# Two chunks of a small projection placed between the chunks of the first input block

## The chip, the cores and the metric

The kernel runs on one core of a Trainium2 chip. The metric is the device time in microseconds of one execution, the median of several runs. The engines are TensorE (PE, with its weight loads listed apart as PEld), VectorE (DVE), ScalarE (ACT), GpSimd (POOL) and SyncE (SP), which here only starts transfers (DMAs).

## The reference

One decoder layer on 256 tokens of width 2048, all in float32:

```
h = rms_norm(x);  proj = h @ w_in            # 2048 x 10536, split into mLSTM, RWKV-7 and gate columns
x = x + rms_norm(merge(mlstm(...), rwkv7(...), gates) @ w_out)
x = x + rms_norm(cross_attention(rms_norm(x), rms_norm(mem)))
x = x + rms_norm((gelu(conv(h @ w_up)[gate]) * conv(h @ w_up)[up]) @ w_down)     # 2048 -> 2 x 8192 -> 2048
```

Of the columns of `w_in`, 296 are a small projection: the low-rank inputs of RWKV's decay, rate and gate (64, 64 and 160 columns) and the 8 gate columns of the mLSTM heads. The rest is a matter of large matrix products.

## The kernel before

**Blocks and chunks.** All large products are cut into blocks, listed in `blocks` in the order in which they run, and each block into chunks along the contraction. In an "fm" block (512 output columns) the weights are the stationary operand and the activations (256 tokens) the moving one; a chunk is two slices of 128 rows, 1024 values on each of the 128 partitions (512 KB). In a "tm" block the activations are stationary. The float32 product is made of three passes with two-part operands: activations high and low (`hh`, `hl`), weights high and low (`wh`, `wl`), as high x high, low x high and high x low. So an fm chunk is 2 x 4 x 3 = 24 matmuls of 256 columns; a chunk of the small projection (block 1, "tm", 296 columns, 8 chunks, 296 KB each) is 12 matmuls of 296 columns.

**Order and indices.** `visits()` lists which chunks of which block run when; the running number of a chunk in that list, `i`, is its index. Before: 0 to 7 the first input block (`w_in` 0), 8 to 15 the small projection, 16 to 71 seven more fm input blocks, 72 to 103 four tm blocks, 104 to 199 gates and branches, 200 to 231 the mixer's output, 232 to 239 the key block of cross-attention, 240 and 241 the first two chunks of its value block, 242 to 249 its query block, 250 to 255 the rest of the value block, 256 to 263 its output block, 264 to 519 the up projection (32 blocks), 520 to 647 the down projection.

**Feed.** `Feed` loads and stages the chunks by index. `dma` starts the load on SP; `hi` casts the chunk to the high part on ACT (L401); `lo` subtracts on DVE (L441). Each index is staged a few indices ahead of its matmuls (`feed.lo(i + 3)`, loads up to `i + 6`). The first eight indices land in a space of their own (`sm`), the others in a ring of four. `begin`, `first` and `second` do the same by hand for the first two chunks, in halves. For the first block the activations themselves are loaded in pieces of two slices (`x_load`, 256 KB each) and split into `hh` and `hl` by `x_piece` (ACT and DVE, L66), called from `pre_r0`. Loads are queued on SP in program order. Each engine works through its instructions in program order too.

**Line place and kicks.** `staged` chooses where in its buffer the staged weights of a chunk start: 16 elements in for fm blocks and for blocks narrower than 512 columns, 0 for wider tm blocks, the two slices `e` elements apart. The table `KICK` displaces single indices by 8 elements: kind 0 the first slice, kind 1 the second, kind 2 both. It costs no instruction.

**Side work.** What is not a chunk (evacuations of finished blocks, statistics, attention, the RWKV recurrence) is written as generators which `Spread` serves in small pieces. Its step, `half()`, is called twice in each chunk; it takes at most one piece of the first-come queue, as a budget for ACT and DVE allows, and the pieces of the "chains", which come each `chain` steps, the first after `phase` steps. Pieces that have matmuls or transposes put them into PE's stream between two half chunks; such an insertion is called a visit here. The first block's evacuation contains the statistic of the first norm; the small block's evacuation ends with six transposes and starts the gates and the low-rank work. `x_tokens` (L1939 to L1948) is a chain that transposes the residual for the final output: 32 transposes of 128 x 128, four to each of eight visits, with one copy by ACT behind each visit, 8 steps (four chunks) apart.

Of the kernel before, what the change touches and what calls it, by code (L numbers as in the profile page):

```python
# [15 lines left out]
P = 128  # L16
# [129 lines left out]
def _layer(ctx, tc, nc, d, dbg):  # L146
    act, dve = Meter(nc.scalar, 200.0, 0.83), Meter(nc.vector, 70.0, 1.04)
    pool, pe, sp = nc.gpsimd, nc.tensor, nc.sync
    side = Spread(act, dve)
# [27 lines left out]
    def aux(name, shape=None):  # L177
        return pp.tile(shape or [P, 512], F32, tag="aux", bufs=4, name=name)
# [157 lines left out]
    blocks = []  # L336

    def block(kind, srcs, xs, evac, before=None, cols=512, pool_=None, pre=None, bankwise=False, tail=0):
# [2 lines left out]
                           pool=pool_ or acc, pre=pre, task=None, bankwise=bankwise, tail=tail))  # L341
        return blocks[-1]

    KICK = {16: 0, 18: 2, 36: 2, 52: 1, 60: 2, 104: 0, 108: 0, 111: 0, 116: 0, 117: 1, 120: 1, 134: 0, 138: 2, 140: 0, 159: 1,
            168: 0, 216: 2, 219: 2, 236: 2, 243: 2, 257: 2, 266: 2}

    HB = [slice(0, 256), slice(256, 512)]

    class Feed:
# [7 lines left out]
        def begin(self):  # L357

            r = self.raw[0] = self.sm[0][:, 0]
            m = KD + S  # L360
            sp.dma_start(xf[:, 0:m], d["xf"][:, 0:m])
            act.dma_start(r[:, 0, HB[0]], self.src[0][:, 0, HB[0]])
            sp.dma_start(r[:, 0, HB[1]], self.src[0][:, 0, HB[1]])
            act.dma_start(r[:, 1], self.src[0][:, 1])
            sp.dma_start(xf[:, m:], d["xf"][:, m:])
            r = self.raw[1] = self.sm[0][:, 1]
            for j in range(2):
                sp.dma_start(xq[1][:, j], d["x"][:, 2 + j])
                sp.dma_start(r[:, j], self.src[1][:, j])
            act.activation(mhalf[:, 0:1], mhalf[:, 0:1], AF.Copy)  # L370
            self.nd = 2

        def dma(self, upto):
            while self.nd <= min(upto, len(self.src) - 1):
                s = self.src[self.nd]
                if self.nd < 8:
                    r = self.sm[self.nd // 4][:, self.nd % 4]
                else:
                    r = wp.tile(list(s.shape), F32, tag="raw", bufs=4, name="raw")
                sp.dma_start(r, s)  # L380
                self.raw[self.nd] = r
                self.nd += 1

        def staged(self, name, r, i):


            k, c = r.shape[1:]
            kick = KICK.get(i)
            e = -(-c // 64) * 64
            o = 0 if c >= 512 and self.kind[i] == "tm" else 16  # L390
            if kick is not None:
                o, e = ((24, e + 24), (o, e + 8), (24, e))[kick]
            w = wp.tile([P, 1024 + 128], F32R, tag=name, bufs=4, name=name)
            return w[:, o:o + k * e].rearrange("p (k c) -> p k c", k=k)[:, :, 0:c]
# [10 lines left out]
        def first(self):  # L405

            r, wh, wl = self.raw.pop(0), self.staged("wh", self.src[0], 0), self.staged("wl", self.src[0], 0)
            for h in HB:
                nc.vector.tensor_copy(wh[:, 0, h], r[:, 0, h])
            for kj in range(2):  # L410
                x_split(0, kj)
                if kj:
                    nc.scalar.copy(wh[:, 1], r[:, 1])
                nc.vector.tensor_sub(wl[:, kj], r[:, kj], wh[:, kj])
            self.st[0] = [wh, wl]

        def second(self):

            r, wh, wl = self.raw.pop(1), self.staged("wh", self.src[1], 1), self.staged("wl", self.src[1], 1)
            for kj in range(2):  # L420
                x_split(1, kj)
                nc.scalar.copy(wh[:, kj], r[:, kj])
                nc.vector.tensor_sub(wl[:, kj], r[:, kj], wh[:, kj])
            self.st[1] = [wh, wl]
            self.ns = self.nl = 2

        def early(self, i):

# [33 lines left out]
    def visits():  # L462

        out = []
        for b in blocks:
            n = len(b["srcs"])
            if b is xv:
                out.append((b, 0, 2))
            elif b is xq_:
                out += [(b, 0, n), (xv, 2, len(xv["srcs"]))]  # L470
            elif b is entry[0]:
                out += [(v, c, c + 1) for c in range(n) for v in entry]
            elif b is not entry[1]:
                out.append((b, 0, n))
        return out

    def run():
        order = visits()
        feed = Feed([("xv" if b is xv else b["kind"], s) for b, c0, c1 in order for s in b["srcs"][c0:c1]])
        feed.begin()  # L480
        for c in range(2, 8):
            x_load(c)
            feed.dma(c)
            if c == 4:
                sp.dma_start(par, d["par"])
        i = 0
        pend, ring = [], []
        for b, c0, c1 in order:
            if c0 == 0:
# [4 lines left out]
                n = (b["cols"] // P + 1) // 2 if b["kind"] == "fm" else 2 * max(1, b["cols"] // 512)  # L494
                b["banks"], b["k"] = [], 0
                for _ in range(n):
# [4 lines left out]
                    o = b["pool"](b["kind"], [P, 2, S] if b["kind"] == "fm" or b is xv else None)  # L501
# [3 lines left out]
            banks, nm, k = b["banks"], b["cols"] // P, b["k"]  # L505
# [5 lines left out]
                srcs, tail = srcs[:-nt], srcs[-nt:]  # L511
            for ci, s in enumerate(srcs):
                if b["pre"]:
                    b["pre"](ci, feed)
                feed.lo(i + 1)
                twin = bool(entry) and ci == 0 and c0 == 0 and b in entry
                if twin and b is entry[0]:
# [7 lines left out]
                wh, wl = feed.st.pop(i)  # L525
                for kj in range(s.shape[1]):
                    xh, xl = b["xs"](k) if kj else ahead
                    first, last = k == 0, k == nk - 1
                    if b["kind"] == "fm":
                        steps = []  # L530
                        for m in range(nm):
                            o = banks[m // 2][:, m % 2]
                            a, c = wh[:, kj, m * P:(m + 1) * P], wl[:, kj, m * P:(m + 1) * P]
# [19 lines left out]
                    else:  # L553
                        for g, o in enumerate(banks):
                            n = o.shape[1]
# [9 lines left out]
            if nt:  # L565
# [10 lines left out]
                n = len(steps)  # L576
# [49 lines left out]
    def x_piece(c):  # L626
        for j in range(2):
            x_split(c, j)
# [4 lines left out]
    def pre_r0(ci, feed):  # L633
        if ci == 0:
            keep_warm(7)
            feed.first()
            feed.second()
            x_piece(2)
            feed.lo(2)
        if ci + 3 < 8:  # L640
            x_piece(ci + 3)
        else:

            for c in range((ci - 5) * 2, (ci - 5) * 2 + 2):
                st0.add(xq[c])
        if ci == 4:
            sp.dma_start(con, d["con"])

    def pre_sm(ci, feed):
        if ci == 0:  # L650
            sp.dma_start(up[0:64], d["w_up"])
        if ci == 1:
            sp.dma_start(up[64:128], d["a_up"])

    M, tasks = {}, {}
# [1192 lines left out]
    def fu_evac(b):  # L1848
        def gen(ps):
# [17 lines left out]

            if b == 0:
                yield from M["res"].wait(30)
                side.add(x_tokens(), chain=8)  # L1870
            dve.tensor_mul(us[0], ps[0], bc(stf.rb, 2))
            yield
            base(0)
# [62 lines left out]
    def x_tokens():  # L1936

        M["xt"] = []
        for f in range(4):  # L1939
            if f % 2 == 0:  # L1940
                M["xt"].append(U("xt", [P, 2, 1024]))
            for t in range(2):
                q = aux("xt", [P, 4, P])
                for j in range(4):
                    k = f * 4 + j
                    pe.transpose(q[:, j], M["xr"][k // 8][:, k % 8, t * P:(t + 1) * P], ident)  # L1946
                act.copy(M["xt"][f // 2][:, t, f % 2 * 512:f % 2 * 512 + 512], q.rearrange("p a b -> p (a b)"))
                yield  # L1948

    def load_gain():  # L1950
        M["gain"] = mp.tile([P, D], F32, tag="hT", bufs=2, name="gain")
# [175 lines left out]
```

## Time and profile before

| | |
|---|---|
| median of 3 runs | 1863.75 us (1863.1 to 1864.75) |
| the profiled execution | 1862.86 us, span 1861.0 us |
| PE / PEld busy | 1851.9 / 1767.3 us |
| DVE / ACT / POOL busy | 1296.2 / 1015.3 / 34.8 us |
| granted TensorE clock | 0.999 |
| read from HBM | 347.01 MB, 188 GB/s over the span |

A row of the timeline is: start in us from the span's start, duration in us, engine, line of the kernel, operation, output tile <- input tiles, shapes, and the number of merged instructions; in brackets idle time of the engine before it and who ended it. `fm` and `tm` are the PSUM tiles of blocks of these kinds. Matmuls are pipelined: the distance from start to start counts, not the duration. Staged weights and the activations have the names `wh`, `wl`, `hh`, `hl` (in later blocks `mh`, `qh`, `fh` and so on). The DMA view lists transfers by line with their size and the median time from issue to landing.

### The profile page before, as it was taken

What the parts mean: (1) busy time and instruction counts of PE and PEld (TensorE: products, weight loads), DVE (VectorE), ACT (ScalarE), POOL (GpSimd) and SP (SyncE); (2) the same over time, 40 slices, a digit from 0 to 9 for tenths busy, and PEclk for the clock granted to TensorE, in tenths of its full rate; (3) what the DMA queues carried; (4) which work ended last, traced back from release to release, by engine and by line L of the source; (5) the groups of instructions that cost most, each with busy time, mean ns of one, the idle gap of its engine ahead of it and who ended that gap; (6) DMA issues with size and microseconds to landing.
All of it is one profiled execution on the core that took longest, in us unless ns stands there. A gap on an engine that the chain in (4) does not pass through costs nothing.

```text
span 1861.0 us, 36212 instructions
## 1 busy us (share of the span) xinstructions
PE 1851.9 (100%) x14930; PEld 1767.3 (95%) x14930; DVE 1296.2 (70%) x1834; ACT 1015.3 (55%) x1493; POOL 34.8 (2%) x64
## 2 busy tenths in 40 slices
PE   9999999999999999999999999999999999999998
PEld 9999888999999999999999999999999988888887
DVE  7889787566676858787766667766666775556555
ACT  6776445555454746666554455444445554545544
POOL 0100020000000000000000000000000000000000
PEclk9999999999999999999999999999999999999999
DMA  7556545455556765555666666666666666666664
GB/s 263 192 174 192 181 153 163 133 164 156 177 190 195 273 203 182 161 183 172 197 196 195 196 193 193 192 193 195 195 196 194 195 193 215 192 193 192 194 192 145
DMA packets 98486, 351.47 MB, mean 189 GB/s; under 512 B 10960, under 2 KB 11984, under 8 KB 97936
## 3 DMA queue, kind: packets, MB, share of 16 engines
q1 hardware_dynamic: 97744, 348.23, 59.8%
q8 instruction: 117, 1.92, 0.4%
q10 hardware_dynamic: 576, 0.92, 0.1%
q14 instruction: 49, 0.40, 0.1%
HBM read 347.01 MB, written 2.10 MB: 188 GB/s over the span
## 4 chain that ended last, share of the span: by engine, by line
PE 99%; DMA 0%; DVE 0%; ACT 0%; issue 0%; DVEq 0%; ACTq 0%
PE fm L181 69%; PE tm L181 25%; DMA w<-in_w_in_dram 0%; PE gram L181 0%; PE Y L181 0%; PE num L181 0%; PE lv L181 0%; PE X L181 0%; PE U L181 0%; PE zg L181 0%; PE zwa L181 0%; PE xsc L181 0%; PE xt L1946 0%; PE stb L181 0%; PE Tn L181 0%; PE xo L181 0%
## 5 line engine op out<-in xcount | busy, mean ns | idle before, releaser
L441 DVE TENSOR_TENSOR wl<-raw,wh 128x1024 fp32r<-128x1024 f32 (+1 forms) x639 | 774.9, 1218 | 415.3 <-ACT wh L401 407.6
L401 ACT CAST wh<-raw 128x1024 fp32r<-128x1024 f32 (+1 forms) x639 | 663.9, 1044 | 472.7 <-PE fm L181 358.7
L181 PE MATMUL fm<-fh,wh 128*128 128x256 f32 x2048 | 565.4, 277 | 0.6 <-DVE fh L66 0.6
L181 PE MATMUL fm<-fl,wh 128*128 128x256 f32 x2048 | 564.4, 277 | 0.0
L181 PE MATMUL fm<-fh,wl 128*128 128x256 f32 x2048 | 564.4, 277 | 0.0
L181 PEld LDWEIGHTS fm<-fh,wh 128*128 128x128 f32 x2048 | 383.9, 188 | 0.8 <-DVE fh L66 0.8
L181 PEld LDWEIGHTS fm<-fl,wh 128*128 128x128 f32 x2048 | 383.8, 188 | 0.0
L181 PEld LDWEIGHTS fm<-fh,wl 128*128 128x128 f32 x2048 | 383.7, 188 | 0.0
L181 PE MATMUL tm<-wh,as 128*128 128x512 f32 x1024 | 315.6, 390 | 0.0
L181 PE MATMUL fm<-hh,wh 128*128 128x256 f32 x1024 | 284.5, 280 | 0.7 <-ACT wh L401 0.6
L181 PE MATMUL fm<-hh,wl 128*128 128x256 f32 x1024 | 282.1, 277 | 0.8 <-DVE wl L441 0.8
L181 PE MATMUL fm<-hl,wh 128*128 128x256 f32 x1024 | 282.0, 277 | 0.0
L181 PEld LDWEIGHTS tm<-wh,as 128*128 128x128 f32 x1024 | 192.2, 188 | 39.9
L181 PE MATMUL tm<-wl,as 128*128 128x512 f32 x512 | 199.5, 390 | 0.0
L181 PEld LDWEIGHTS fm<-hh,wh 128*128 128x128 f32 x1024 | 192.2, 189 | 1.7 <-ACT wh L401 0.8
L181 PEld LDWEIGHTS fm<-hh,wl 128*128 128x128 f32 x1024 | 191.5, 188 | 1.0 <-DVE wl L441 1.0
L181 PEld LDWEIGHTS fm<-hl,wh 128*128 128x128 f32 x1024 | 191.7, 188 | 0.1
L181 PEld LDWEIGHTS tm<-wl,as 128*128 128x128 f32 x512 | 96.1, 188 | 19.9
L66 ACT CAST as<-ac 128x256 fp32r<-128x256 f32 x128 | 45.6, 404 | 110.8 <-PE tm L181 110.8
L66 DVE TENSOR_TENSOR as<-ac,as 128x256 fp32r<-128x256 f32 x128 | 48.6, 421 | 61.7 <-ACT as L66 61.7
L181 PE MATMUL fm<-mgh,wh 128*128 128x256 f32 x256 | 71.1, 278 | 0.0
L181 PE MATMUL fm<-mgl,wh 128*128 128x256 f32 x256 | 70.9, 277 | 0.0
(411 smaller groups left out, 2224.5 us busy)
## 6 DMA issues: line engine op xcount, KB each, us to landing
raw<-in_w_fu_dram SPq DMA_DIRECT2D x256, 512.0 KB, 4.3
raw<-in_w_in_dram SPq DMA_DIRECT2D x152, 512.0 KB, 3.5
raw<-in_w_fd_dram SPq DMA_DIRECT2D x128, 512.0 KB, 4.0
raw<-in_w_br_dram SPq DMA_DIRECT2D x32, 512.0 KB, 4.2
raw<-in_w_mo_dram SPq DMA_DIRECT2D x32, 512.0 KB, 3.8
raw<-in_w_xk_dram SPq DMA_DIRECT2D x8, 512.0 KB, 3.6
raw<-in_w_xv_dram SPq DMA_DIRECT2D x8, 512.0 KB, 3.6
raw<-in_w_xq_dram SPq DMA_DIRECT2D x8, 512.0 KB, 4.0
```

The source lines that it names most:

```text
L66: return f(out, *a, **k)
L181: pe.matmul(out, lhsT, rhs, start=start, stop=stop, skip_group_check=True)
L401: nc.scalar.copy(wh, r)
L441: nc.vector.tensor_sub(wl, r, self.st[self.nl][0])
```

## The change

The first two chunks of the small projection move from indices 8 and 9 to 1 and 3: the order is now first block's chunk 0, small 0, chunk 1, small 1, chunks 2 to 7, small 2 to 7. From index 16 on all is as before. The loads, the casts and the splitting of x are reordered to match; the loads now run up to index 9 in `run` (the first eight indices' space holds the smaller chunks too). The small chunks' staged weights start at 0 instead of 16 elements. `con` and `up` are loaded at the same chunks of their blocks.

In `KICK` four entries go to the index ahead (138 to 137, 216 to 215, 236 to 235, 243 to 242; all of kind 2) and one is new (282).

`x_tokens` makes eight transposes and two copies in each of four visits, 16 steps apart, the first 24 steps after the point where it was before.

```diff
-    KICK = {..., 134: 0, 138: 2, 140: 0, 159: 1,
-            168: 0, 216: 2, 219: 2, 236: 2, 243: 2, 257: 2, 266: 2}
+    KICK = {..., 134: 0, 137: 2, 140: 0, 159: 1,
+            168: 0, 215: 2, 219: 2, 235: 2, 242: 2, 257: 2, 266: 2, 282: 2}
...
-            r = self.raw[1] = self.sm[0][:, 1]
+            self.nd = 1
+            self.dma(1)
+            r = self.raw[2] = self.sm[0][:, 2]
             for j in range(2):
                 sp.dma_start(xq[1][:, j], d["x"][:, 2 + j])
-                sp.dma_start(r[:, j], self.src[1][:, j])
+                sp.dma_start(r[:, j], self.src[2][:, j])
...
-            self.nd = 2
+            self.nd = 3
...
-            o = 0 if c >= 512 and self.kind[i] == "tm" else 16
+            o = 0 if self.kind[i] == "tm" else 16
...
-            if b is xv:
+            if b is blocks[0]:
+                out += [(b, 0, 1), (blocks[1], 0, 1), (b, 1, 2), (blocks[1], 1, 2), (b, 2, n)]
+            elif b is blocks[1]:
+                out.append((b, 2, n))
+            elif b is xv:
...
+        feed.dma(3)
         for c in range(2, 8):
             x_load(c)
-            feed.dma(c)
+            feed.dma(c + 2)
...
-            feed.second()
-            x_piece(2)
-            feed.lo(2)
-        if ci + 3 < 8:
-            x_piece(ci + 3)
+            feed.lo(1)
+            feed.second()
+            feed.lo(3)
+        elif ci < 5:
+            x_piece((0, 3, 5, 6, 7)[ci])
...
     def pre_sm(ci, feed):
-        if ci == 0:
+        if ci < 2:
+            x_piece(2 + 2 * ci)
+        if ci == 2:
             sp.dma_start(up[0:64], d["w_up"])
-        if ci == 1:
+        if ci == 3:
...
-                side.add(x_tokens(), chain=8)
+                side.add(x_tokens(), chain=16, phase=24)
...
-            for t in range(2):
-                q = aux("xt", [P, 4, P])
+            qs = [aux("xt", [P, 4, P]) for _ in range(2)]
+            for t, q in enumerate(qs):
                 for j in range(4):
                     k = f * 4 + j
                     pe.transpose(q[:, j], M["xr"][k // 8][:, k % 8, t * P:(t + 1) * P], ident)
+            for t, q in enumerate(qs):
                 act.copy(M["xt"][f // 2][:, t, f % 2 * 512:f % 2 * 512 + 512], q.rearrange("p a b -> p (a b)"))
-                yield
+            yield
```

More of the change, by code (lines that the diff above doesn't have):

```diff
@@ L342, in block @@
         return blocks[-1]
-    KICK = {16: 0, 18: 2, 36: 2, 52: 1, 60: 2, 104: 0, 108: 0, 111: 0, 116: 0, 117: 1, 120: 1, 134: 0, 138: 2, 140: 0, 159: 1,
-            168: 0, 216: 2, 219: 2, 236: 2, 243: 2, 257: 2, 266: 2}
+    KICK = {16: 0, 18: 2, 36: 2, 52: 1, 60: 2, 104: 0, 108: 0, 111: 0, 116: 0, 117: 1, 120: 1, 134: 0, 137: 2, 140: 0, 159: 1,
+            168: 0, 215: 2, 219: 2, 235: 2, 242: 2, 257: 2, 266: 2, 282: 2}
     HB = [slice(0, 256), slice(256, 512)]
@@ L376, in dma @@
                 if self.nd < 8:
-                    r = self.sm[self.nd // 4][:, self.nd % 4]
+                    r = self.sm[self.nd // 4][:, self.nd % 4].rearrange("p k c -> p (k c)")
+                    r = r[:, 0:2 * s.shape[2]].rearrange("p (k c) -> p k c", k=2)
                 else:
@@ L415, in first @@
             self.st[0] = [wh, wl]
+            self.ns = self.nl = 1
         def second(self):
-            r, wh, wl = self.raw.pop(1), self.staged("wh", self.src[1], 1), self.staged("wl", self.src[1], 1)
+            r, wh, wl = self.raw.pop(2), self.staged("wh", self.src[2], 2), self.staged("wl", self.src[2], 2)
             for kj in range(2):
@@ L423, in second @@
                 nc.vector.tensor_sub(wl[:, kj], r[:, kj], wh[:, kj])
-            self.st[1] = [wh, wl]
-            self.ns = self.nl = 2
+            self.st[2] = [wh, wl]
+            self.ns = self.nl = 3
         def early(self, i):
@@ L513, in run @@
                 if b["pre"]:
-                    b["pre"](ci, feed)
+                    b["pre"](c0 + ci, feed)
                 feed.lo(i + 1)
```

## The prediction

> **What bounds the kernel now.** I read the page first, for the engine that sets the span.
>
> ```profile
> span 1861.0 us, 36212 instructions
> PE 1851.9 (100%) x14930; PEld 1767.3 (95%) x14930; DVE 1296.2 (70%) x1834; ACT 1015.3 (55%) x1493; POOL 34.8 (2%) x64
> ```
>
> TensorE (PE) is busy for all but 9.1 us of 1861.0. Neither the matmuls nor their sizes are changed, so the change can only win or lose in PE's idle time and in the distance from one matmul's start to the next. The profiled execution took 1862.86 us, 1.86 us around its span, and the median of the runs shown is 1863.75, 0.89 us above it; the sum is made at 1862.86, and 0.89 us are added at the end.
>
> Next I read the timeline of the first 17 us, PE, ScalarE (ACT) and VectorE (DVE) apart, to find the idle time that the reordering can reach.
>
> ```profile
> 7.89 0.28 PE L181 MATMUL fm<-hh,wh 128*128 128x256 f32 x1
> ...
> 10.15 0.62 PE L181 MATMUL fm<-hh,wl 128*128 128x256 f32 x4
> 11.35 0.38 PE L181 MATMUL fm<-hh,wh 128*128 128x256 f32 x1 [0.58 <-ACT wh L401]
> 11.57 0.28 PE L181 MATMUL fm<-hl,wh 128*128 128x256 f32 x1
> 12.61 0.38 PE L181 MATMUL fm<-hh,wl 128*128 128x256 f32 x1 [0.76 <-DVE wl L441]
> ...
> 15.23 0.28 PE L181 MATMUL fm<-hh,wh 128*128 128x256 f32 x1
> ```
> ```profile
> 7.96 0.62 ACT L422 CAST wh<-w 128x512 fp32r<-128x512 f32 x1 [0.28 <-DMA w<-in_w_in_dram]
> ...
> 10.25 1.05 ACT L401 CAST wh<-w 128x1024 fp32r<-128x1024 f32 x1 [0.35 <-DMA w<-in_w_in_dram]
> ...
> 14.68 1.05 ACT L401 CAST wh<-w 128x1024 fp32r<-128x1024 f32 x1 [0.25 <-DMA w<-in_w_in_dram]
> ```
> ```profile
> 11.33 1.23 DVE L441 TENSOR_TENSOR wl<-w,wh 128x1024 fp32r<-128x1024 f32 x1 [0.92 <-ACT wh L401]
> ```
>
> The row at 7.89 is the first matmul of chunk 1 of the first input block, 11.35 that of chunk 2, 15.23 that of chunk 3. Chunk 2 waits twice: for its weights' cast, and at its third matmul for the subtraction. The cast at 10.25 itself waited for the transfer. From 10.25 a fixed chain runs to the third matmul at 12.61 (1.05 us cast, 1.23 us subtraction, some 0.08 between), 2.36 us. So **DMA sets the time up to 12.61**; after that PE runs without a stop while the casts still follow the transfers. The windows say the same (stretch, length, busy time of PE, PEld, DVE, ACT and POOL with counts, granted clock, DMA share, GB/s):
>
> ```profile
> 5.00:10.00 5.00, 4.91 (x41) 4.70 (x41) 4.25 (x9) 3.88 (x8) 0.00 (x0) 1.00 0.97 315
> 10.00:15.00 5.00, 3.66 (x30) 3.26 (x29) 3.78 (x7) 4.05 (x7) 0.00 (x0) 1.00 1.02 393
> ```
>
> DMA is full (0.97, 1.02), PE is not (3.66 of 5 us), and the granted clock is 1.00.
>
> **Part one, the small chunks moved forward.** Everything stands against the price of one small chunk, and of its casting:
>
> ```profile
> 28.83 0.30 PE L181 MATMUL tm<-wh,hh 128*128 128x296 f32 x1
> ...
> 30.43 0.29 PE L181 MATMUL tm<-wh,hh 128*128 128x296 f32 x1
> ```
> ```profile
> L441 DVE TENSOR_TENSOR wl<-raw,wh 128x592 fp32r<-128x592 f32 x4 | 3.1, 769 | 0.0
> ...
> L401 ACT CAST wh<-raw 128x592 fp32r<-128x592 f32 x4 | 2.7, 675 | 0.4 <-PE fm L181 0.4
> ```
>
> Twelve matmuls in 1.60 us, fed by 296 KB; a chunk of the input block takes 24 matmuls and needs 768 KB (512 of weights, 256 of x). Two small chunks bring PE 3.20 us of work that x chunk 0 and 1 already allow, and 592 KB that are queued on SP ahead of chunk 2. Two chunks' worth, 1536 KB, came between the casts at 10.25 and 14.68 (4.43 us, 347 KB/us), one chunk's 768 KB between 7.96 and 10.25 (335 KB/us). At 341 KB/us the 592 KB cost 1.73 us: the cast of chunk 2 moves from 10.25 to 11.98, and its third matmul to 11.98 + 2.36 = 14.34. Is PE there by then? From 7.89: small chunk 1.60, chunk 1 2.72 (the later spacing of 24 matmuls, priced below), small chunk 1.60 gives 13.81, two matmuls later 14.04. It still waits 0.3 us, once. From the third matmul to chunk 3 the trace has 15.23 - 12.61 = 2.62 us, so chunk 3 starts at 16.96, with 3.20 us of the later work done: as if at 13.76 instead of 15.23. **Gain 1.47 us.** Without the remaining wait it would be 1.77, and with the 0.1 us of restart (0.38 us for the matmul at 12.61 against 0.28) some 1.9. If the extra bytes come at the 315 GB/s of the window, 606 thousand bytes take 1.92 us and the gain is 1.28; if the small pieces land half a microsecond later still, some 0.8. I take 1.47.
>
> What else this step issues: the cast and subtraction of the first small chunk (0.68 and 0.77 us) come ahead of chunk 1's x and weights on ACT and DVE. Chunk 1's last weights, cast at 7.96 now, land 296/341 = 0.87 us later, at 8.83; cast 0.62 us and subtraction of like size end near 10.1, and PE needs that half at 7.89 + 1.60 + 1.36 = 10.85: covered. The chunks 3 and 4 of the block are cast one visit later in program order, but their transfers still lead PE: the cast of chunk 4, at 14.68 now, goes to 16.4 and its subtraction ends near 18.7, before 16.96 + 2.72 = 19.68. The loads of con, up and the other small chunks are queued later on SP, behind the block's own weights, for uses after 19 us. No wait is added beyond the one at 14.34.
>
> The Trainium skill, SBUF — State Buffer, section "The DMA setup-cost knee", gives 436 GB/s as the asymptote of large transfers; by it the 606 thousand bytes cost an estimated 1.39 us, no wait but a few hundredths is left, and the part would give 1.8 us.
>
> **Part two, the line place of the small chunks.** Their staged weights start at offset 0 instead of 16 elements, for all eight. No row has that form. Bounds: at the pace of the input blocks (2.72 us for 24 x 256 columns) 296 columns take 0.131 us against 1.60/12 = 0.133, a gain of 0.2 us over 96 matmuls; at the slow spacing described next, 4% dearer, a loss of 0.5. I take 0, nearest to a row that has the same shape.
>
> **Part three, the kick table.** An entry displaces one chunk's staged weights by 8 elements. What it acts on is seen by the first matmuls of successive chunks: rows of the cross-attention query block (indices 242 to 244 and the one behind), of the mixer's gates (137, 138, 139), of the key block (235, 236, 237), and chunk 18 with 19:
>
> ```profile
> 730.52 0.28 PE L181 MATMUL fm<-qh,wh 128*128 128x256 f32 x1
> ...
> 733.35 0.28 PE L181 MATMUL fm<-qh,wh 128*128 128x256 f32 x1
> ...
> 736.17 0.28 PE L181 MATMUL fm<-qh,wh 128*128 128x256 f32 x1
> ...
> 738.88 0.28 PE L181 MATMUL fm<-qh,wh 128*128 128x256 f32 x1
> ```
> ```profile
> 428.22 0.39 PE L181 MATMUL fm<-hh,wh 128*128 128x256 f32 x1
> ...
> 431.17 0.28 PE L181 MATMUL fm<-hh,wh 128*128 128x256 f32 x1
> ...
> 433.98 0.28 PE L181 MATMUL fm<-hh,wh 128*128 128x256 f32 x1
> ```
> ```profile
> 710.90 0.28 PE L181 MATMUL fm<-mh,wh 128*128 128x256 f32 x1
> ...
> 714.11 0.28 PE L181 MATMUL fm<-mh,wh 128*128 128x256 f32 x1
> ...
> 716.92 0.28 PE L181 MATMUL fm<-mh,wh 128*128 128x256 f32 x1
> ```
> ```profile
> 48.78 0.28 PE L181 MATMUL fm<-hh,wh 128*128 128x256 f32 x1
> ...
> 51.67 0.28 PE L181 MATMUL fm<-hh,wh 128*128 128x256 f32 x1
> ```
>
> Nothing waits in these stretches, yet 24 matmuls take 2.83, then 2.82 (the chunk with the kick), then 2.71. **There are two spacings**, 0.113 and 0.118 us; a visit of other matmuls or a change of block can leave PE in the slow one, 0.11 us a chunk, and a kicked chunk ends it. At 242 the kick now sits on the first slow chunk instead of the second: 2.83 + 2.82 becomes 2.82 + 2.71, gain 0.12. At 137 the slow chunk has a visit in front (2.95); a kicked chunk behind a visit takes 2.94 (172.18 to 175.12, quoted below), so 137 stays and 138 goes from 2.81 to 2.72: 0.09. I give 215 the same 0.09 as an estimate, being built like 137. At 235 the visit falls in the middle: 3.21 us, with a fast first half. A kick in fast spacing is dear (chunk 18: 51.67 - 48.78 = 2.89, 0.17 over 2.72), half of it 0.085, so 235 loses what 236 (2.81) wins: 0. The new one at 282 replaces the visit that ended the slow spacing there: 0. Sum 0.30; bounds 0 (the early kick doesn't hold and the slow spacing goes on, then more is lost, see the rivals) and 0.4.
>
> **Part four, the transposes.** Eight visits of four become four visits of eight, from chunk 295 instead of 283 on.
>
> ```profile
> 868.16 0.60 PE L1946 MATMUL xt<-con,xr 128*128 128x128 f32 x4
> 868.52 0.37 PE L181 MATMUL fm<-fh,wh 128*128 128x256 f32 x1
> 868.73 0.28 PE L181 MATMUL fm<-fl,wh 128*128 128x256 f32 x1
> 868.85 0.28 PE L181 MATMUL fm<-fh,wl 128*128 128x256 f32 x1
> 868.96 0.28 PE L181 MATMUL fm<-fh,wh 128*128 128x256 f32 x1
> ```
> ```profile
> 171.39 1.03 PE L1057 MATMUL vt<-con,vT 128*128 128x128 f32 x8
> 172.18 0.36 PE L181 MATMUL fm<-hh,wh 128*128 128x256 f32 x1
> ...
> 175.12 0.29 PE L181 MATMUL fm<-hh,wh 128*128 128x256 f32 x1
> ```
>
> The return to the stream costs 0.21 instead of 0.113 us, 0.10 a visit, the same behind four transposes as behind eight (172.18 against 868.52). Four visits less: **0.39 us**. ACT copies 2 x 0.59 us at once, with the whole up projection as cover, and the results are wanted only at the very end. The two PSUM banks of a visit are free, because the third block, which holds two of that pool, is evacuated before chunk 295.
>
> **Sum.** 1.47 + 0 + 0.30 + 0.39 = 2.16 us: 1862.86 - 2.16 = 1860.70, and with 0.89 a median of **1861.6**. That is 0.12% faster; a measurement of this kernel can tell about 0.2% (3.7 us) from no change.
>
> **Rivals.**
>
> *Eight transposes leave PE slow for good* (slower). The place is chunk 295; the price 0.11 us a chunk up to 519, 225 chunks, 24.8 us; it decides as soon as 20 chunks stay slow, since 20 x 0.11 eats the sum. For it: the old visit of eight at 171.39 is followed by a kicked chunk, and the new visits have no kick behind them. Against it: the four old visits that end on the second token half, as every new one does (868.16 is one), fall back to fast spacing within two matmuls (0.12, then 0.11). 1861.6 + 24.8 = 1886. Chance 0.06. If each visit turns the spacing over, two stretches of eight chunks cost 1.8: 1863.4, counted in the next.
>
> *Side work slides.* The first input block ends two chunks later, so its evacuation starts four steps of the side schedule later, and what queues behind it (the small block's transposes, the gates, the low-rank products) comes two to three steps later:
>
> ```profile
> 46.74 0.60 PE L690 MATMUL smT<-con,smw 128*128 128x128 f32 x4
> ```
>
> This sits in chunk 17 and would go to 18. The kicks at 18, 36 and 52 stay. If the last low-rank product, now in front of 36's kick, comes behind it, the spacing is slow from 37 to 52: 15 chunks, 1.7 us, so 1863.3. Chance 0.18. For it: the kicks are fixed to indices. Against: a visit can as well end the slow spacing.
>
> *The front gains little*, if the small pieces land late or the first small chunk isn't cast by 7.89: with 0.5 instead of 1.47, 1862.6. Chance 0.09.
>
> *Each small transfer costs a whole latency.*
>
> ```profile
> xf<-in_xf_dram SPq DMA_DIRECT2D x1, 136.0 KB, 2.8
> ```
>
> Alone on an empty queue 136 KB took 2.8 us. If two small loads each held up the queue so long, chunk 2 would be cast at 15.85 instead of 11.98, 3.9 us later: 1865.5. Against it: the queue is full at 393 GB/s with eight loads in flight. Chance 0.03. The Trainium skill, same section, has about 2 us of fixed cost for each transfer and advises large ones; by its fit two loads would cost an estimated 5.4 us one after the other. The trace's full DMA share speaks against adding them.
>
> *All goes better*: no wait left, 0.2 from the line place, 0.17 from a kick at 18 that becomes useful: near 1860.0 and below. Chance 0.06.
>
> **How the numbers follow.** The forecast has 0.58: 1860.7 to 1862.6. The range 1860.0 to 1864.6 takes in the slide and the weak front, leaves out the two slow ends (0.09) and about 0.08 below. Faster by more than 0.2% needs 1860.0: 0.08. Slower than 1867.5: 0.06 for the lasting slow spacing and 0.02 for a slide without an end, 0.08. Within: 0.84.
>
> **What would show it.** Chunk 2's third matmul near 14.3 with one wait of 0.3 us on the subtraction, chunk 3 near 17.0; four visits of eight transposes about 18 us apart from some 890 us on, and 2.72 us for the chunks between; 138, 216, 236 and 243 at 2.72. It would be wrong if slow spacing runs through dozens of chunks, or if chunk 3 starts after 18 us.

## The result, and the profile after

| | before | after |
|---|---|---|
| median of 4 runs each, same chip | 1864.25 us (1863.10 to 1864.89) | 1891.53 us (1891.07 to 1892.57) |
| the profiled execution | 1862.86 us, span 1861.0 | 1892.57 us, span 1890.8 |
| PE / PEld busy | 1851.9 / 1767.3 us | 1880.0 / 1795.5 us |

The ratio is **1.0148, interval 1.013 to 1.0165**: slower by 27.3 us. The prediction was 1861.6 us with a range up to 1864.6. It was wrong.

The head of the page after:

```profile
span 1890.8 us, 36215 instructions
PE 1880.0 (99%) x14930; PEld 1795.5 (95%) x14930; DVE 1296.6 (69%) x1834; ACT 1019.0 (54%) x1493; POOL 34.8 (2%) x64
```

The number of matmuls is the same and PE is "busy" for 28.1 us longer. So most of the loss is not idle time; the same matmuls stand farther apart. To place it, the start of the same chunk is compared in the two timelines (the index is the one of the new order; up to index 10 the order differs, from there on each index is the same chunk):

| from the first matmul of ... to that of ... | after minus before, us |
|---|---|
| start to 10 | -1.44 |
| 10 to 16 | +0.74 |
| 16 to 18 | **+5.60** |
| 18 to 137 | +0.04 |
| 137 to 141 | +0.15 |
| 141 to 235 | -0.07 |
| 235 to 250 | **+1.02** |
| 250 to 282 | -0.04 |
| 282 to 520 | **+23.82** |
| 520 to the end | -0.02 |

They add up to 29.80, the difference of the two spans. The medians differ by 27.3 only: the profiled execution after is the slowest of its four, and the one before is faster than the four it was measured with. Three places (in bold) lose the time; the front gains as forecast.

**The front.** PE's timeline after at chunk 2 (14.27), chunk 3 (16.98) and index 10 (30.59), and ACT's at the cast of chunk 2:

```profile
14.27 0.28 PE L181 MATMUL fm<-hh,wh 128*128 128x256 f32 x1
...
14.49 0.28 PE L181 MATMUL fm<-hh,wl 128*128 128x256 f32 x1
...
16.98 0.28 PE L181 MATMUL fm<-hh,wh 128*128 128x256 f32 x1
...
30.59 0.30 PE L181 MATMUL tm<-wh,hh 128*128 128x296 f32 x1
```
```profile
11.99 1.05 ACT L404 CAST wh<-w 128x1024 fp32r<-128x1024 f32 x1 [0.43 <-DMA w<-in_w_in_dram]
```

The cast is at 11.99, chunk 2 runs without a wait and chunk 3 starts at 16.98.

**A new wait at chunk 16.** PE's waits (engine, tile, line, releaser; us in total, times, longest), its timeline there, and DVE's:

```profile
PE fm L181 <- DVE pr L66: 3.2, 2, 2.8
```
```profile
41.84 0.36 PE L181 MATMUL fm<-hh,wh 128*128 128x256 f32 x1 [0.42 <-DVE pr L66]
...
45.58 0.55 PE L181 MATMUL fm<-hh,wh 128*128 128x256 f32 x1 [2.78 <-DVE pr L66]
...
46.14 0.41 PE L181 MATMUL fm<-hh,wl 128*128 128x256 f32 x1
46.36 0.41 PE L181 MATMUL fm<-hh,wh 128*128 128x256 f32 x1
...
50.84 0.39 PE L181 MATMUL fm<-hh,wh 128*128 128x256 f32 x1
```
```profile
41.01 0.68 DVE L66 TENSOR_TENSOR pr<-fm,st_b 128x512 f32<-128x512 f32 x1
...
43.61 1.23 DVE L445 TENSOR_TENSOR wl<-raw,wh 128x1024 fp32r<-128x1024 f32 x1 [0.45 <-ACT wh L404]
44.75 0.68 DVE L66 TENSOR_TENSOR pr<-fm,st_b 128x512 f32<-128x512 f32 x1
```

`pr<-fm,st_b` reads a PSUM bank of the first block. The rows at 41.01 and 44.75 end at 41.69 and 45.43, and each is followed 0.15 us later by a matmul of chunk 16 that had waited. Before, the same two rows of DVE were at 37.35 and 41.09, and the first matmul of chunk 16 at 42.54:

```profile
37.35 0.68 DVE L66 TENSOR_TENSOR pr<-fm,st_b 128x512 f32<-128x512 f32 x1
...
41.09 0.69 DVE L66 TENSOR_TENSOR pr<-fm,st_b 128x512 f32<-128x512 f32 x1
```
```profile
42.54 0.28 PE L181 MATMUL fm<-hh,wh 128*128 128x256 f32 x1
```

The second ended at 41.78: 0.76 us to spare. Both are 3.66 us later now. The code says why a matmul depends on them: the fm and tm blocks take their banks from a ring of four, and a new bank needs the evacuation of the block that had it four banks ago. The first block and the small one hold four banks between them, so the next block's banks are the first block's.

```python
                    if b["pool"] is acc:
                        if len(ring) >= 4:
                            side.need(ring[-4]["task"])
                        ring.append(b)
```

After the wait the matmuls are 0.21 to 0.22 us apart (46.14 to 46.36) until 50.84. The window from 45 to 50 us, after first and then before, gives the reason in the granted clock (the third number from the end):

```profile
45.00:50.00 5.00, 4.42 (x21) 4.45 (x22) 2.54 (x4) 3.61 (x10) 0.00 (x0) 0.50 0.33 108
```
```profile
45.00:50.00 5.00, 5.00 (x46) 5.00 (x45) 3.81 (x4) 3.50 (x9) 0.53 (x1) 1.00 0.76 222
```

The clock was 0.50 where it had been 1.00. Of the 5.60 us lost from 16 to 18 the wait makes 2.94 (42.52 to 45.58 from start to start, instead of 0.12), and the 25 distances behind it, 0.10 dearer each, make 2.5; some 0.1 is in restarts. The wait of 0.42 us in front of chunk 16 is in the row 10 to 16. The Trainium skill, TensorE: Matmul & The Clock Gate, section "What's actually happening", has the clock fall to half after an idle window of about 3.4 us and come back after about 3.4 us of sustained work. Half the clock agrees (0.50), the durations do not quite: here a wait of 2.78 us was enough, and PE worked 5.26 us (45.58 to 50.84) before the spacing recovered.

**The spacing from 295 to 519.** A visit of eight after, the chunk behind it, and the last chunk of the up projection; then the same 200 us of both kernels, after first:

```profile
895.45 1.04 PE L1957 MATMUL xt<-con,xr 128*128 128x128 f32 x8
896.24 0.36 PE L181 MATMUL fm<-fh,wh 128*128 128x256 f32 x1
896.44 0.28 PE L181 MATMUL fm<-fl,wh 128*128 128x256 f32 x1
...
899.27 0.28 PE L181 MATMUL fm<-fl,wh 128*128 128x256 f32 x1
...
1532.13 0.28 PE L181 MATMUL fm<-fh,wh 128*128 128x256 f32 x1
...
1534.95 0.63 PE L181 MATMUL tm<-wh,as 128*128 128x512 f32 x2
```
```profile
1100.00:1300.00 200.00, 200.00 (x1701) 200.00 (x1700) 134.03 (x179) 97.69 (x125) 0.00 (x0) 1.00 0.62 186
```
```profile
1100.00:1300.00 200.00, 200.00 (x1767) 200.00 (x1766) 138.27 (x185) 100.16 (x128) 0.00 (x0) 1.00 0.65 195
```

From the second matmul of chunk 295 (896.44) to that of 296 (899.27) are 2.83 us, and the last chunk still takes 2.82 (1532.13 to 1534.95). In 200 us there are 1701 matmuls instead of 1767, 0.1176 us each instead of 0.1132, with PE full, the clock at 1.00 and the DMA share lower. Over 225 chunks of 24 that is 225 x 24 x 0.0044 = 23.8 us. The slow stretch starts behind the first visit of eight: the visit is the cause to be tested.

### The profile page after: what moved, and what is told of

Its sections match the earlier page's. It is cut to its first block, busy times and chain, and to the rows that moved or that the text cites. A ratio compares the mean times of both kernels' runs of the same rounds, so it can differ in the third digit from the quotient of the medians.

```text
span 1890.8 us, 36215 instructions
## 1 busy us (share of the span) xinstructions
PE 1880.0 (99%) x14930; PEld 1795.5 (95%) x14930; DVE 1296.6 (69%) x1834; ACT 1019.0 (54%) x1493; POOL 34.8 (2%) x64
## 4 chain that ended last, share of the span: by engine, by line
PE 99%; DVE 0%; ACT 0%; issue 0%; DVEq 0%; POOL 0%; POOLq 0%
PE fm L181 70%; PE tm L181 25%; PE gram L181 0%; PE Y L181 0%; PE num L181 0%; PE lv L181 0%; PE X L181 0%; PE U L181 0%; PE zg L181 0%; PE zwa L181 0%; DVE wl L445 0%; PE xsc L181 0%; PE xt L1957 0%; PE warm L181 0%; PE Tn L181 0%; PE xo L181 0%
## 5 line engine op out<-in xcount | busy, mean ns | idle before, releaser
L445 DVE TENSOR_TENSOR wl<-raw,wh 128x1024 fp32r<-128x1024 f32 x639 | 775.9, 1219 | 443.8 <-ACT wh L404 437.7
L404 ACT CAST wh<-raw 128x1024 fp32r<-128x1024 f32 x639 | 664.9, 1045 | 502.5 <-PE fm L181 386.4
L181 PE MATMUL fm<-fh,wh 128*128 128x256 f32 x2048 | 572.9, 281 | 0.6 <-DVE fh L66 0.6
L181 PE MATMUL fm<-fh,wl 128*128 128x256 f32 x2048 | 572.2, 280 | 0.0
L181 PE MATMUL fm<-fl,wh 128*128 128x256 f32 x2048 | 572.2, 280 | 0.0
L181 PEld LDWEIGHTS fm<-fh,wh 128*128 128x128 f32 x2048 | 390.7, 191 | 0.8 <-DVE fh L66 0.8
```

Source lines behind the costliest of these rows:

```text
L181: pe.matmul(out, lhsT, rhs, start=start, stop=stop, skip_group_check=True)
L404: nc.scalar.copy(wh, r)
L445: nc.vector.tensor_sub(wl, r, self.st[self.nl][0])
```

## The experiments

A shift below is the start of a chunk in the kernel's timeline minus that of the same chunk before. The first 32 us differ by up to 3.5 us between executions of the same code (see the end), so stretches are compared, not totals. Most variants ran once; what is read from them are distances inside their timelines. "Slow" is a chunk of 2.82 us or more, "fast" one of 2.72; behind a visit the count starts at the second matmul.

**1. The transposes alone.** Before, with the new `x_tokens` and the entry 282.

```diff
-            168: 0, 216: 2, 219: 2, 236: 2, 243: 2, 257: 2, 266: 2}
+            168: 0, 216: 2, 219: 2, 236: 2, 243: 2, 257: 2, 266: 2, 282: 2}
...
-                side.add(x_tokens(), chain=8)
+                side.add(x_tokens(), chain=16, phase=24)
...
-            for t in range(2):
-                q = aux("xt", [P, 4, P])
+            qs = [aux("xt", [P, 4, P]) for _ in range(2)]
+            for t, q in enumerate(qs):
...
-                yield
+            yield
```

> The kernel before with only the transposes of the change (four visits of eight, 16 steps apart, 24 steps later) and the new kick at 282. Theory A (a visit of eight leaves PE in the slow spacing and no later visit of eight ends it): slow from chunk 295 to 519, 225 chunks x 0.112 = 25.2 us, less some 1.4 us for the visits and slow chunks saved before 295: span near 1884.8 against 1861.0 before. Rival B (the slow spacing in the changed kernel came from elsewhere, such as the reordered front): chunks of 2.72 us, span near 1860.6.

Measured: 1888.4 us (before on the same chip 1863.81). The shift is +1.78 at 282 and +25.60 at 520: 23.8 us, as in the changed kernel, and slow from 295 to 519.

```profile
891.23 1.04 PE L1946 MATMUL xt<-con,xr 128*128 128x128 f32 x8
...
892.23 0.28 PE L181 MATMUL fm<-fl,wh 128*128 128x256 f32 x1
...
895.05 0.28 PE L181 MATMUL fm<-fl,wh 128*128 128x256 f32 x1
```

Second matmul to second matmul, 2.82. So this part alone makes 23.8 of the 29.8 us, without the front and the other kicks.

**2. The same places, four at a time.** As 1, but the visits of before (four transposes each, eight visits), 16 steps apart from the same first place. Against the kernel before:

```diff
-            168: 0, 216: 2, 219: 2, 236: 2, 243: 2, 257: 2, 266: 2}
+            168: 0, 216: 2, 219: 2, 236: 2, 243: 2, 257: 2, 266: 2, 282: 2}
...
-                side.add(x_tokens(), chain=8)
+                side.add(x_tokens(), chain=16, phase=24)
```

> The kernel before with the visits of four transposes kept, eight of them, but spaced and delayed as in the change (16 steps, 24 steps later), and the kick at 282. Theory A (the count of transposes in a visit decides): fast spacing after every visit, span 1861.0 - 0.4 = 1860.6. Rival C (place and distance of the visits decide): slow after the visit at 295, span up to 1885.

Measured: 1864.44 us; the shift is 1.69 at 282 and 1.68 at 520.

```profile
913.37 0.60 PE L1946 MATMUL xt<-con,xr 128*128 128x128 f32 x4
...
913.92 0.28 PE L181 MATMUL fm<-fl,wh 128*128 128x256 f32 x1
...
916.65 0.28 PE L181 MATMUL fm<-fl,wh 128*128 128x256 f32 x1
```

2.73 us behind a visit, and fast behind each of the eight. The later place and the wider distance cost nothing; it is what a visit holds.

**3. The token halves exchanged.** As 1, but the visit ends on the first token half.

```diff
-            for t, q in enumerate(qs):
+            for t, q in reversed(list(enumerate(qs))):
```

> As x8_alone, the two token halves exchanged inside each visit, so that the first half comes last. Theory A (the count decides): slow as in x8_alone, span near 1884.8. Rival E (the addresses of the last transposes decide): another spacing than x8_alone; fast would be a span near 1860.6.

Measured: 1890.33 us, slow from 295 to 519 as in 1; from 282 to 520 again 23.8 us (3.74 to 27.56). Which half the last transposes read does not decide here. That they read the second half was the prediction's argument against its first rival.

**4. A kick at each visit of eight.** As 1, with four more entries.

```diff
-            168: 0, ..., 282: 2}
+            168: 0, ..., 282: 2, 295: 0, 303: 0, 311: 0, 319: 0}
```

> As x8_alone, with a kick of kind 0 on each chunk behind a visit of eight (295, 303, 311, 319). Theory A (the visit puts PE into the slow spacing, a kick ends it): four slow chunks, 0.10 us each, then fast; four stalls of 0.09 saved, so within 0.3 us of the kernel before, span 1860.4 to 1861.0. Rival D (a kick does not hold here): slow to 519, span near 1885.

Measured: 1866.71 us; from 282 to 520 +1.77 instead of 23.8, but more than the 0.3 expected: 295 and 311, which PE reached fast, stayed slow up to the next visit, while 303 and 319, which it reached slow, were ended by their entries.

```profile
891.60 1.04 PE L1946 MATMUL xt<-con,xr 128*128 128x128 f32 x8
...
892.59 0.28 PE L181 MATMUL fm<-fl,wh 128*128 128x256 f32 x1
...
895.44 0.28 PE L181 MATMUL fm<-fl,wh 128*128 128x256 f32 x1
...
898.26 0.28 PE L181 MATMUL fm<-fl,wh 128*128 128x256 f32 x1
```

Chunk 295, with the entry, 2.85; chunk 296 still 2.82. A visit of eight with a kick behind it can be cured, but not by a kick just anywhere.

**5. The kick a chunk later.** As 1, with `296: 2, 304: 0, 312: 2, 320: 0`.

> As x8_alone, with kicks one chunk behind each visit of eight: kind 2 at 296 and 312, kind 0 at 304 and 320. Theory M (a kick ends the slow spacing when its chunk begins in settled slow spacing, whatever the kind, and fails on the first chunk behind a visit): fast from 297, 305, 313 and 321 on; each visit then costs 0.28 to 0.30 us in place of two of 0.10, so chunk 520 stands 0.2 to 0.5 us later than in the kernel before, counted from chunk 282. Rival N (kind 0 or kind 2 alone holds): slow after two of the four visits, 0.8 to 22 us more.

Measured: 1866.84 us; from 282 to 520 +1.2, where 0.2 to 0.5 was expected. The idea that a kick in a settled slow stretch always ends it fell: 296 did not. The visit at 303 came into a slow stretch and left it fast, the one at 311 left a fast stretch fast, the one at 319 left it slow, and there the kick at 320 held. The two visits of eight that left PE fast show that eight transposes do not always do harm.

**6. How many.** Before, with 29 extra visits in the up projection, three chunks apart, of 4, 1, 4, 2, 4, 3 and so on transposes. They are work that nobody reads; the computation is otherwise whole.

```diff
+                side.add(probes(), chain=6, phase=80)
...
+    def probes():
+        for n in [4, 1, 4, 2, 4, 3, 4, 5, 4, 6, 4, 7, 4, 8, 4, 8, 4, 7, 4, 6, 4, 5, 4, 3, 4, 2, 4, 1, 4]:
+            qs = [aux("pb", [P, 4, P]) for _ in range(-(-n // 4))]
+            for j in range(n):
+                pe.transpose(qs[j // 4][:, j % 4], M["xr"][0][:, j % 4, j // 4 * P:(j // 4 + 1) * P], ident)
+            yield
```

> The kernel before with 29 further visits of transposes in the up projection, whose results nobody reads, three chunks apart from about chunk 323 on: visits of four between visits of 1, 2, 3, 5, 6, 7, 8, 8, 7, 6, 5, 3, 2, 1. Theory P (the count of transposes decides): both visits of one count end alike, fours always fast, eights slow, and a slow stretch lasts three chunks (24 matmuls at 0.118 us each) until the next four. Rival Q (the state before, or something finer such as the phase of the waits, decides): the two visits of one count differ, or a four does not end a slow stretch.

Measured (the time, 1879.19 us, holds the extra work and says nothing):

| transposes in the visit | 1 | 2 | 3 | 4 | 5 | 6 | 7 | 8 |
|---|---|---|---|---|---|---|---|---|
| visits that left PE fast, of all | 0/2 | 1/2 | 2/2 | 15/15 | 2/2 | 2/2 | 1/2 | 0/2 |

```profile
978.33 0.27 PE L1955 MATMUL pb<-con,xr 128*128 128x128 f32 x1
...
978.56 0.28 PE L181 MATMUL fm<-fl,wh 128*128 128x256 f32 x1
...
981.38 0.28 PE L181 MATMUL fm<-fl,wh 128*128 128x256 f32 x1
...
986.92 0.60 PE L1955 MATMUL pb<-con,xr 128*128 128x128 f32 x4
...
987.49 0.28 PE L181 MATMUL fm<-fl,wh 128*128 128x256 f32 x1
...
990.21 0.28 PE L181 MATMUL fm<-fl,wh 128*128 128x256 f32 x1
```

One transpose: 2.82 us for the chunk behind it; four: 2.72, and the slow stretch is over. All six slow stretches that a visit of another size began were ended by the next visit of four. So the number counts, and a longer visit is not a worse one (1 is as bad as 8, 5 and 6 are good). All visits but those of four came into a fast stretch. With 2 and 7 differing between their two visits, the number is not the whole rule.

**7. The front alone.** The changed kernel with the kick table, the line place and `x_tokens` of before.

```diff
...
-            o = 0 if self.kind[i] == "tm" else 16
+            o = 0 if c >= 512 and self.kind[i] == "tm" else 16
...
-                side.add(x_tokens(), chain=16, phase=24)
+                side.add(x_tokens(), chain=8)
...
```

The parts not shown put `KICK` and the body of `x_tokens` back to those of before.

> The kernel before with only the order of the first ten chunks changed (line place, kicks and transposes as before). Theory F (the front gains about 1.4 us up to chunk 10, then chunk 16 waits for the first block's PSUM banks, whose evacuation starts four steps later, and the clock falls to half behind the wait): chunk 18 starts 4 to 5 us later than before, span 1864.5 to 1866.5. Rival G (the wait came from the slower small chunks with their new line place): no wait, span near 1859.6.

Measured: 1868.23 us; the shift is -1.16 at 10, -0.63 at 16, +5.12 at 18, +5.05 at 72. The wait is there with the clock behind it:

```profile
PE fm L181 <- DVE pr L66: 3.1, 2, 2.8
```
```profile
45.00:50.00 5.00, 4.35 (x20) 4.38 (x21) 2.58 (x4) 3.54 (x10) 0.00 (x0) 0.50 0.36 108
```

The same kernel in 3 rounds:

> The order of the front alone, timed. Theory F: the gain of 1.2 to 1.4 us up to chunk 10 is given back with the wait at chunk 16 and the half clock behind it: 4 to 5 us slower than the kernel before, near 1868.5. Rival (the wait comes from the profiled execution alone): 1862 to 1863.

1867.5 us (1865.81 to 1869.04) against 1864.18, ratio 1.0013 with the interval 1.0004 to 1.0023. The reorder alone makes the kernel slower: by 3.3 us between the medians, by 0.7 to 4.3 by the interval, less than the 4 to 5 expected. The profiled execution of this round has the wait too, and a shift of +6.05 at 72.

**8. Other banks for the small block.** As 7, the small block's banks from the other pool, so that block 2 need not wait for the first block's.

```diff
-    block("tm", [d["w_sm"][c] for c in range(8)], xs0, sm_evac, cols=296, pre=pre_sm)
+    block("tm", [d["w_sm"][c] for c in range(8)], xs0, sm_evac, cols=296, pre=pre_sm, pool_=aux)
```

> As front_only, with the small block's two PSUM banks taken from the other pool, so that chunk 16 finds two free banks. Theory F: no wait at chunk 16, no fall of the clock, the gain of the front stays: chunk 18 starts 1.2 to 1.9 us earlier than before, span 1859.1 to 1859.8. Rival G, or a wait for something else than the banks: chunk 16 still waits for VectorE, span above 1863.

Measured: 1864.39 us; the shift is -0.78 at 16 and -0.76 at 17 (no wait), but +0.08 at 18 and +1.41 at 72. The side work is late all the same: the six transposes behind the small block wait for ACT, the weights of chunk 23 come 0.5 us late, and 24 to 28 are slow. Timed, with the expectations

> The front with the small block's banks in the other pool, timed. Theory F: the wait is gone, the gain of the front stays, less the slow stretches seen in its profile between chunks 17 and 28 (some 1.5 us): within 1 us of the kernel before, 1862.8 to 1864.8. If the banks are not the cause: near 1868.

1864.85 us, ratio 1.0005 (0.9996 to 1.0014). A variant that also drops the entry 18 and moves 216 to 215,

> As front_aux, without the kick at 18 (0.17 us dear where the spacing is fast) and with 216 moved to 215 (0.08 us). 0.25 us less than front_aux if nothing else follows: 1862.5 to 1864.5. If the slow spacing then runs on from 18, up to 3.7 us more (to chunk 36, 18 x 0.11 = 2.0, or to 52).

came to 1864.64 us, 1.0001 (0.9991 to 1.0011). Its profiled execution was the slowest of its ten, 1869.19 us: PE waited up to 2.2 us for ACT at those six transposes, and the clock fell to 0.50 (50 to 55 us). Neither version beats the kernel before. Free banks take 2.65 us off the 1867.5 of experiment 7; the late side work is left.

**9. The evacuation made earlier.** As 7, with four steps fewer in the statistic that the evacuation waits for (`finish(n)` lets n steps pass twice).

```diff
-        yield from st0.finish(3)
+        yield from st0.finish(1)
```

> front_only with the two pauses in the statistic of the first norm cut from three steps to one, so that the first block's evacuation ends as early as before although it starts four steps later. Theory F (the late evacuation makes the wait at chunk 16): no wait there, no fall of the clock, the front's gain stays: 1.0 to 2.5 us faster than the kernel before, 1861.7 to 1863.2. If the wait has another cause: near 1867.5 as front_only.

Measured, 5 rounds: **1862.37 us** (1861.74 to 1864.35) against 1863.63, ratio 0.9995 (0.9987 to 1.0004). There is no wait at 16: the two reads of the banks are at 36.49 and 40.23, and the clock stays at 1.00.

```profile
36.49 0.69 DVE L66 TENSOR_TENSOR pr<-fm,st_b 128x512 f32<-128x512 f32 x1
...
40.23 0.68 DVE L66 TENSOR_TENSOR pr<-fm,st_b 128x512 f32<-128x512 f32 x1
```
```profile
41.67 0.28 PE L181 MATMUL fm<-hh,wh 128*128 128x256 f32 x1
```
```profile
45.00:50.00 5.00, 5.00 (x45) 5.00 (x44) 3.53 (x6) 3.23 (x6) 0.53 (x1) 1.00 0.88 271
```

The shift is -1.76 at 10, -0.87 at 16 (the statistic's own visit now waits some 0.7 us), and stays: -0.79 at 520. With both cures,

> As front_fin1, with the small block's banks in the other pool. Theory F: the same as front_fin1 within 0.5 us, since one of the two cures is enough. If part of the wait remained in front_fin1, this one is faster by it.

1862.39 us, 0.9993 (0.9984 to 1.0002): the second adds nothing, and beside experiment 8 the earlier evacuation also removes the late side work. The wait at chunk 16 and the low clock behind it are thus caused by the late evacuation of banks that chunk 16 needs; either cure removes them. The version is 1.26 us below the kernel before, but its interval includes 1.

**10. The line place alone.** Before with `o = 0 if self.kind[i] == "tm" else 16`.

> The kernel before with only the line place of the small chunks changed (0 instead of 16 elements). From the changed kernel's small chunks (1.65 us for 12 matmuls instead of 1.60): 8 x 0.05 = 0.4 us more, span 1861.4. Rival (the 1.65 us came from their place between other chunks): span 1861.0 within 0.1.

Measured: 1863.93 us. From 8 to 16 the shift goes from +0.15 to +0.51: 0.36 us for eight small chunks, as expected. A slow stretch at 25 to 27, 0.37 us, followed a matmul that was 0.05 us late; whether the line place has to do with it was not tried.

**11. The kicks alone.** Before with `137: 2`, `215: 2`, `235: 2`, `242: 2` in place of 138, 216, 236 and 243.

> The kernel before with only the four moved entries of the kick table. Theory K (a kick on the chunk that has the visit, or the change of block, in it or just ahead does not hold, one on the next does): slow from 235 to 249 and from 137 to 140, fast behind 215: 1.0 + 0.1 - 0.1 us, span 1862.0. Rival L (the lost kicks of the changed kernel hang on its other parts): the sum of the prediction, 0.3 us less, span 1860.7.

Measured: 1867.29 us, of which 3.16 are in its first 30 us, where the code is that of before. By stretches: 137 to 141 +0.16, 215 to 218 -0.06, 235 to 250 +1.02. That is what the changed kernel shows (+0.15, -0.05, +1.02).

The parts, each alone, add up: 5.05 (front, at 72) + 1.05 (kicks, 72 to 258) + 23.8 (transposes) = 29.9, against 29.8 us between the two spans. That they agree to 0.1 us is partly chance: the second trace of the front alone has 6.05 for the 5.05, and the line place (0.36) is in none of the three.

## Why the prediction was wrong

The measured time is 27 us above the upper end of the range. Three steps failed: a late evacuation was given no wait, the moved kicks were taken to hold, and the lasting slow spacing behind eight transposes was held to be all but excluded.

**Part one, the front: right in the price of the loads, in part lucky in the gain, wrong in one sentence.** The cast of chunk 2 was put at 11.98 and came at 11.99; chunk 3 at 16.96, and came at 16.98; the gain was put at 1.47, and at index 10 it was 1.44. The one wait of 0.3 us at chunk 2 did not appear. PE arrived later, with the third matmul at 14.49 instead of 14.34, since eight distances in chunk 0 were 0.21 us (+0.38 at index 1) and a small chunk took 1.64 instead of 1.60; from there to chunk 3 it needed 2.49 instead of 2.62. That these two cancel is luck. In the seven other traces with the new order the gain at index 10 is between 0.25 and 1.76 us, and the trace of before is itself an early one of its order. Two small loads in a full queue cost their bytes and no more: the cast moved 1.74 us for 592 KB. The rule of the Trainium skill (SBUF — State Buffer, "The DMA setup-cost knee"), about 2 us fixed for each transfer, would have made it some 5.4 us by the prediction's own estimate; with eight loads in flight the trace shows none of that. The section's 436 GB/s, which it calls the limit of the SBUF side and not of HBM, gives an estimated 1.39 us, too fast by 0.35. (The 136 KB load from which the prediction took a whole latency was not quite alone in its 2.8 us: ACT started another load at the same 0.74 us.)

What failed is "No wait is added beyond the one at 14.34". The prediction had followed the loads, casts and splits, and asked of the late evacuation only what queues *behind* it. It did not ask who needs what the evacuation *frees*. Block 2 takes the first block's banks. The slack was 0.76 us in the trace of before (41.78 to 42.54), the delay 3.66. Of this, 1.76 is the later end of the first block (28.83 to 30.59). Most of the rest lies on DVE between the copy of the statistic and the first read, after first:

```profile
38.22 0.42 DVE L66 COPY st_b<-stb 128x256 f32<-128x256 f32 x1
39.87 1.23 DVE L445 TENSOR_TENSOR wl<-raw,wh 128x1024 fp32r<-128x1024 f32 x1 [1.23 <-ACT wh L404]
```
```profile
36.33 0.42 DVE L66 COPY st_b<-stb 128x256 f32<-128x256 f32 x1 [0.52 <-PE stb L181]
36.67 0.77 DVE L441 TENSOR_TENSOR wl<-raw,wh 128x592 fp32r<-128x592 f32 x1
```

The copy is 1.89 us later. Before, the subtraction of a small chunk stood between it and the read at 37.35 (1.02 us from copy to read); after, that of a chunk of the next block, which itself waits for its cast (2.79 us to the read at 41.01). In experiment 9 it is a small chunk again, and 1.03 us. The wait itself would have cost 3.2 us; the low clock behind it, which no row of before shows, nearly doubled that. Experiments 7 and 9 show both.

**Part two, the line place: mis-sized.** Put at 0, with bounds from a gain of 0.2 to a loss of 0.5; experiment 10 measured a loss of 0.36. The upper bound is not worked out like the lower: at the slow spacing (2.83 us for 24 x 256 columns) 296 columns take 0.136 us, and 96 matmuls lose 0.29. By that bound 0.36 lies outside.

**Part three, the kicks: wrong in sign.** 0.30 was to be gained with a bound of 0 below; 1.1 was lost. After, chunks 138 and 236:

```profile
436.12 0.28 PE L181 MATMUL fm<-hh,wh 128*128 128x256 f32 x1
...
438.95 0.28 PE L181 MATMUL fm<-hh,wh 128*128 128x256 f32 x1
...
719.23 0.28 PE L181 MATMUL fm<-mh,wh 128*128 128x256 f32 x1
...
722.06 0.28 PE L181 MATMUL fm<-mh,wh 128*128 128x256 f32 x1
```

Both take 2.83 where 2.72 was forecast. The step that failed is the one at 137 and 235, that a kick one chunk earlier still ends the slow stretch. At 235 it comes in the fast first half, the visit behind it makes PE slow, and nothing ends that until 249: the entry at 242 met a stretch that was already slow and did not hold either. 215 held, for 0.05 instead of 0.09. The lower bound should have been the length of the stretch that the entry at 236 ended, since a misplaced kick costs all of it; the text had said "then more is lost" and carried no number to the sum.

**Part four, the transposes: wrong, and the rival had it.** The first rival, a lasting slow spacing at 24.8 us and 1886, is what happened: 23.8 us in experiment 1. It had a chance of 0.06. The evidence "for" was the better: all six visits of eight transposes of 128 x 128 in the trace of before (149.56, 171.39, 340.42, 357.15, 416.38 and 499.37 us) have an entry in the kick table for the chunk that they fall in or that starts behind them. The evidence "against" took the address of the last operand for what decides, from visits of four only. Experiment 1 refutes it, since its visits end on the second token half too and stay slow; experiment 3 shows that the other half does no better.

The small term was mis-sized as well. The return to the stream costs 0.20 us behind eight as behind four (896.24 to 896.44), as said. But from the first transpose to the first matmul behind the visit, eight take 0.79 us (895.45 to 896.24; 171.39 to 172.18 in the prediction's own rows), and two times four take 2 x 0.36 (868.16 to 868.52). That takes back 0.07 of the 0.10 saved in each pair: four visits fewer are worth some 0.1 us, not 0.39. The visits also stand 23.5 us apart and not 18, since 16 steps are eight chunks.

**Side work slides** was right in that the evacuation comes later, and looked in the wrong place. The small block's transposes stayed in chunk 17 (51.65 us, in a chunk from 49.56 to 53.68), and chunks 35 to 37, around the kick of 36, take what they took before; the damage came at chunk 16. The range ended at 1864.6, and the two mechanisms missed are 5.6 and 23.8 us.

## What to carry to other kernels

When a block of work is moved, ask of each late piece not only what stands behind it in its queue but what buffers it frees and who takes them; a slack of under 1 us in front of a bank (0.76 here) is a price to be put in the sum, with the low clock that can follow the wait (2.5 us here). Where a trace shows the same matmuls at two spacings, and a change alters what precedes long stretches, the rival is worth the whole stretch (225 chunks here) and its chance should be taken from forms that the trace has shown, not from a likeness. A change that can lose so much should be tried on its own before it is joined with a gain of 1 us.

## What the runs showed of the hardware

The spacing of otherwise equal matmuls, 0.1132 or 0.1176 us with the granted clock at 1.00 and no wait, lasted in the changed kernel over 225 chunks, to the end of the up projection; which one follows depends on the work that touched PE before. In the up projection four fp32 transposes left it fast in 31 of 31 visits (experiment 2, the kernel before, experiment 6), one in none of 2, eight in 2 of 22. It does not hold everywhere: in the value block of the kernel before the visit of four at 762.90 us came into a slow stretch and left it slow (763.46 to 764.64 for ten distances), while those at 767.03 and 771.56 left it fast. What decides stays open.

From its first transpose to the matmul behind it a visit of one took 0.03 us, of four 0.36, of eight 0.79 (experiment 6): 0.109 for each transpose but the last, which the next matmul follows at once.

A wait of 2.78 us halved the clock for more than 5 us. The length of the wait alone does not decide: in experiment 4 waits of 1.19 and 0.76 us at chunk 2 were followed by granted clocks of 0.90 and 0.76 (10 to 15 and 15 to 20 us), and in experiment 1 waits of 1.85 and 0.76 us at the same place by 1.00. This is one reason why the first 32 us vary with unchanged code: index 10 started between 31.96 and 35.41 us in the traces with the old order. A row of experiment 3 at 15 to 20 us, where the kernel before has a clock of 1.00, shows it too:

```profile
15.00:20.00 5.00, 5.00 (x32) 5.00 (x32) 4.73 (x8) 4.41 (x8) 0.00 (x0) 0.66 1.04 402
```
